# Recurrent mixer: hierarchy steps over both decays in one instruction, prefix sums in place, double tiles in turn

## The chip, the cores and the metric

The kernel runs on one core of a Trainium2 chip, as one program launched once. The time is that of the device, in microseconds (us), from runs of the whole program. Its engines work from queues of their own: TensorE (PE, with its weight loads PEld), VectorE (DVE), ScalarE (ACT), GpSimd (POOL) and SyncE (SP), which issues transfers. They wait for each other through semaphores.

## The reference, cut to what matters

The program is an encoder trunk of two layers over 1024 tokens of width 1024. Layer 0 mixes tokens by windowed attention, layer 1 by a bidirectional gated linear recurrence (HGRN2) with 8 heads; each layer also has four heads of cross-attention and ends in a channel mixer (ConvGLU). The change touches the recurrence alone:

```python
def gla_chunked(q, k, v, log_f):            # HG_CHUNK = 16
    b = jnp.cumsum(log_f, axis=2)           # prefix sums in a chunk
    b_end = b[:, :, -1:]
    q_dec = q * jnp.exp(b)
    k_dec = k * jnp.exp(-b)
    k_end = k * jnp.exp(b_end - b)
    s = jnp.where(causal, jnp.einsum('bcthk,bcshk->bchts', q_dec, k_dec), 0.0)
    o_intra = jnp.einsum('bchts,bcshv->bcthv', s, v)
    # and then a scan over the chunks: state = decay * state + k_end^T v, o_inter = q_dec state

def mixer_hgrn2(...):
    q, i, zf, zb, gate, xq = jnp.split(u @ w_in, ...)
    f = lb + (1.0 - lb) * jax.nn.sigmoid(z)       # forget gate; its log is log_f, and k = 1 - f
    o = gla_chunked(q, k_f, v, lf_f) + flip_t(gla_chunked(flip_t(q), flip_t(k_b), flip_t(v), flip_t(lf_b)))
    o = rmsnorm(o, norm_g) * jax.nn.silu(gate)
```

## The kernel before

The recurrent mixer is the function `hgrn`. It works by head (8), and in each head by four *directions*: forward and backward, each over two halves of 512 tokens (`direction(h, r, d, b, ...)`, order (0,0), (1,1), (0,1), (1,0)). A head's 128 key channels lie on the partitions, its 512 tokens along the columns. Beside it, on PE, runs the projection of a later head (`proj`): q and the two gates by channel (`proj_fm`, 24 matmuls of 512 columns for a tile `pj`), and values with their output gates by token for two heads at once (`proj_tm`, eight tiles, emptied into `v` by DVE at L1127 and into `gs` by three ACT passes, L1105 to L1107, and a DVE product, L1129). Tiles `pj` are two in turn: the next but one can start only when a tile is empty. `fp32r` weights are split into a high and a low part by ACT (`wh`) and DVE (`wl`, L79), and each product is three matmuls (L83 to L85). Cross-attention units are strewn between (`cross`).

A direction goes like this. ACT makes the log of the gate and of k from the projection `s` (L1191 to L1195). DVE subtracts (L1196), sums prefixes within 16 tokens (`B`, L1198, a scan with a mask that restarts it), and takes the rest to the chunk's end (`R`, L1201). ACT makes EP = exp(B) and ER = exp(R) (L1205, L1206), and exp(-R) and exp(-B) for half of the columns each (L1218, L1219). Four DVE products with q and k (L1220 to L1223) fill two tiles E1 and E2 for the score blocks of 32. Then comes a hierarchy: `step(n)` makes decays over 2n tokens from those over n, one instruction for the half of ER that is earlier in each pair of blocks (L1233) and one for the half of EP that is later (L1234). After the steps of 16 and 32 tokens a tile G (of 32 and of 64) is filled, one half by POOL (L1241, EP times q), the other by DVE (L1242, ER times k). PE then makes the score blocks `pa` (L1226) from G, E1, E2 and G32: 8 matmuls of 64 columns and 24 of 32, each recorded as two. A third step follows, then POOL takes `dec` and `qin` from EP (L1259, L1261), DVE makes ER times k (L1262) and copies the masked scores (L1263), PE transposes ER (`pt`, L1272), ACT copies it (L1274), PE makes the state updates `pu` (L1277), and DVE carries the state on (L1286). After four directions `output` makes the head's result (`po`, L1301).

Tiles: a pool `early` holds five tiles `E` of 512 columns in turn, which serve as a_, L1, R, B, E1, E2, G32 and G64 of each direction, and two EP and two ER.

The order of each engine's instructions is set when the program is built, by a scheduler that reads the order of the code, priorities and its own costs. `with tc.high_priority(AHEAD)` puts the emptying of projection tiles and the score blocks ahead. When an instruction's cost or the tiles that it waits for change, the order changes on all engines.

## Time and profile before

| | us |
|---|---|
| median of three runs (2657.53 to 2662.38) | 2660.64 |
| the profiled execution | 2656.7 |
| its span, first to last instruction | 2654.6 |
| PE busy in the span | 2598.7 |
| DVE busy | 1818.1 |
| ACT busy | 1377.3 |
| POOL busy | 472.4 |
| first and last hierarchy step (L1233) of the mixer start at | 1245.9 and 1889.2 |

The mean granted TensorE clock is 0.999 of full. The profile shows one execution. A group's row gives line, engine, operation, tiles (out<-in), shape and count, then busy us, mean ns of one, and the engine's idle time before them with what ended it. In a row by source line three numbers with strokes are the shortest, the median and the longest duration in ns. Matmuls are pipelined, and their ends are modelled: in a run without a wait they start closer together than they last.

### The profile page before, as it was taken

Reading aid. Unit: us, or ns where it says so; the run is one execution under the profiler, and the core shown is the slowest. Engines: PE = TensorE matmul, PEld = TensorE weight load, DVE = VectorE, ACT = ScalarE, POOL = GpSimd, SP = SyncE. Lnnn points to the kernel's source line nnn. Section 1 sums busy time; section 2 is a strip of 40 time slices with the busy share of each in tenths; the row PEclk is TensorE's granted clock in tenths of the full one; section 3 lists DMA queues with packets and bytes.
Section 4 is the critical chain, followed back from the end, with each engine's and each line's share of the span. In section 5 each row is a group of like instructions: output and inputs, shape, how many; then the busy total and the mean of one; then the engine's idle time right before and its main releaser. Section 6 shows DMA issues by size and latency. Waiting matters only on the chain. (4 is left out here: it accounts for less than half of the span.)

```text
span 2654.6 us, 39112 instructions
## 1 busy us (share of the span) xinstructions
PE 2598.7 (98%) x14420; PEld 2184.3 (82%) x14420; DVE 1818.1 (68%) x3043; ACT 1377.3 (52%) x2503; POOL 472.4 (18%) x520
## 2 busy tenths in 40 slices
PE   8999999999999999999999999999999999999998
PEld 7888887788888888887888888888887788888887
DVE  6688886577655565478688686886757755656447
ACT  6467676545444445454465554555534444445443
POOL 0421010211111100031224131231311111110013
PEclk9999999999999999999999999999999999999999
DMA  9782232367777857674235351103437778785656
GB/s 354 246 174 58 74 91 81 107 190 192 200 202 193 209 154 257 191 251 150 84 112 150 81 128 53 52 25 100 141 105 197 194 191 211 197 202 168 224 192 238
DMA packets 195728, 425.93 MB, mean 160 GB/s; under 512 B 20048, under 2 KB 56272, under 8 KB 189904
## 3 DMA queue, kind: packets, MB, share of 16 engines
q1 hardware_dynamic: 161552, 324.06, 37.7%
q0 software_dynamic: 24544, 90.19, 16.3%
q10 hardware_dynamic: 9440, 9.19, 1.1%
q8 instruction: 113, 1.85, 0.3%
q14 instruction: 79, 0.65, 0.1%
HBM read 330.04 MB, written 116.39 MB: 168 GB/s over the span
## 5 line engine op out<-in xcount | busy, mean ns | idle before, releaser
L89 DVE TENSOR_TENSOR wl<-st,wh 128x1024 fp32r<-128x1024 f32 (+1 forms) x238 | 262.7, 1110 | 317.0 <-ACT wh L88 289.0
L88 ACT CAST wh<-st 128x1024 fp32r<-128x1024 f32 (+1 forms) x238 | 222.4, 936 | 287.2 <-PE X L592 189.7
L83 PE MATMUL pj<-uh,wh 128*128 128x512 f32 x512 | 202.8, 396 | 3.8 <-DVE q L1143 1.8
L592 PE MATMUL X<-wl,wh 128*128 128x512 f32 x528 | 204.6, 389 | 0.0
L592 PE MATMUL X<-wh,wl 128*128 128x512 f32 x528 | 204.5, 389 | 0.0
L85 PE MATMUL pj<-uh,wl 128*128 128x512 f32 x512 | 202.0, 395 | 0.0
L84 PE MATMUL pj<-ul,wh 128*128 128x512 f32 x512 | 201.9, 394 | 0.1
L592 PE MATMUL X<-wh 128*128 128x512 f32 x528 | 198.7, 390 | 1.0 <-ACT c L1006 1.0
L83 PE MATMUL pj<-wh,uh 128*128 128x384 f32 (+1 forms) x512 | 189.3, 371 | 4.7 <-DVE gs L1129 2.5
L85 PE MATMUL pj<-wh,ul 128*128 128x384 f32 (+1 forms) x512 | 187.2, 366 | 0.0
L84 PE MATMUL pj<-wl,uh 128*128 128x384 f32 (+1 forms) x512 | 186.6, 364 | 0.0
L79 DVE TENSOR_TENSOR wl<-st,wh 128x1024 fp32r<-128x1024 f32 (+1 forms) x91 | 115.2, 1272 | 29.3 <-ACT wh L78 28.6
L592 PE MATMUL V<-uh,wh 128*128 128x512 f32 x336 | 130.7, 389 | 0.0
L592 PE MATMUL V<-ul,wh 128*128 128x512 f32 x336 | 130.7, 389 | 0.0
L592 PE MATMUL V<-uh,wl 128*128 128x512 f32 x336 | 130.7, 389 | 0.0
L78 ACT CAST wh<-st 128x1024 fp32r<-128x1024 f32 (+1 forms) x97 | 97.8, 1014 | 46.1 <-PE pj L84 24.2
L592 PEld LDWEIGHTS X<-wh 128*128 128x128 f32 x528 | 99.1, 188 | 22.0 <-ACT c L1006 1.4
L83 PEld LDWEIGHTS pj<-uh,wh 128*128 128x128 f32 x512 | 96.3, 188 | 24.0 <-DVE q L1143 2.6
L592 PEld LDWEIGHTS X<-wl,wh 128*128 128x128 f32 x528 | 99.1, 188 | 20.5
L592 PEld LDWEIGHTS X<-wh,wl 128*128 128x128 f32 x528 | 99.1, 188 | 20.4
L975 POOL TENSOR_TENSOR c<-c,g 128x512 f32<-128x512 f32 x24 | 43.4, 1824 | 388.5 <-DMA st<-hid 159.7
L84 PEld LDWEIGHTS pj<-ul,wh 128*128 128x128 f32 x512 | 96.3, 188 | 18.6 <-DVE ul L89 0.4
(413 smaller groups left out, 7221.8 us busy)
## 6 DMA issues: line engine op xcount, KB each, us to landing
st<-hid SPq DMA_DIRECT2D x154, 256.0 KB, 3.0
st<-in_ffw_dram SPq DMA_DIRECT2D x108, 256.0 KB, 3.4
w2s<-in_ffw_dram POOLq DMA_DIRECT2D x24, 1024.0 KB, 8.7
st<-in_ffw_dram SPq DMA_DIRECT2D x46, 512.0 KB, 4.4
hid<-tt SPq DMA_DIRECT2D x88, 256.0 KB, 4.7
st<-w2s SPq DMA_DIRECT2D x88, 256.0 KB, 3.0
sx<-in_ffw_dram SPq DMA_DIRECT2D x84, 256.0 KB, 3.9
sy<-in_ffw_dram SPq DMA_DIRECT2D x42, 512.0 KB, 7.1
```

What stands on the lines that cost most here:

```text
L78: act.copy(h[:, :n], raw)
L79: (eng or dve).tensor_tensor(l[:, :n], raw, h[:, :n].bitcast(F32), op=ALU.subtract)
L83: pe.matmul(o, ah, bh, start=first, stop=False)
L84: pe.matmul(o, ah, bl, start=False, stop=False)
L85: return pe.matmul(o, al, bh, start=False, stop=last)
L88: act.copy(h, src)
L89: dve.tensor_tensor(l, src, h.bitcast(F32), op=ALU.subtract)
L592: last = pe.matmul(o, x, y, start=new, stop=e, skip_group_check=not first)
L975: pool.tensor_tensor(y[q][:, t, :], y[q][:, t, :], g3[:, c], op=ALU.mult)
```

## The change

Both decays of a direction, and the logs that they are made from, move into one double tile `RP` of 2 x 512 columns, ER ahead of EP; two such tiles take turns. The tiles L1 and a_ are its two halves, the scan writes where it reads, and R is written over L1 with its sign turned (L1209 takes B less its end), so that ER is exp(-R).

`across(x, n)` is an operand over both halves: the earlier half of each pair of n-blocks of ER, and then the later half of each in EP. With it a step is one instruction of 512 columns (L1234 of the new kernel) in place of two of 256. `mixed` is the matching order in E1 and E2. These are filled by two exponentials of 512 columns with opposite sign (L1214, L1215) ahead of EP and ER, which are made in place (L1216, L1217), and then by two products of 512 columns (L1218, L1219) in place of four of 256 and two exponentials of 256.

E1 with E2, and G32 with G64, are halves of double tiles `E`, two in turn. The pool takes 16 KB of a partition where it took 18.

PE has the same matmuls, POOL and SP the same instructions. DVE has 160 fewer, ACT as many as before. Every engine's order in the mixer is another. After line 1181 the new kernel's line numbers are its own; from L1234 on they are one above those of before.

```diff
-            gf = early.tile([P, 512], F32, tag="E", bufs=5, name="gf")
+            gf = early.tile([P, 2, 512], F32, tag="E", bufs=2, name="gf")[:, 0, :]
...
-            def E():
-                return early.tile([P, 512], F32, tag="E", bufs=5, name="E")
+            def pair_of(tag):
+                return early.tile([P, 2, 512], F32, tag=tag, bufs=2, name=tag)
...
+            def across(x, n):
+                return bass.AP(x.tensor, x.offset + er * n, [list(x.ap[0]), [512 + (lt - er) * n, 2], [2 * n, 256 // n], [1, n]])
+            def mixed(x):
+                return bass.AP(x.tensor, x.offset + er * 16, [list(x.ap[0]), [(lt - er) * 16, 2], [32, 16], [1, 16]])
-            a_, L1 = E(), E()
+            RP = pair_of("RP")
+            ER, EP = RP[:, 0, :], RP[:, 1, :]
+            a_, L1 = EP, ER
             act.activation(a_, k, AF.Exp, scale=-1.0)
             act.activation(L1, a_, AF.Ln, bias=1.0)
...
             dve.tensor_tensor(a_, a_, L1, op=ALU.subtract)
-            R, B = E(), E()
-            dve.tensor_tensor_scan(B[:, rev], smask, a_[:, rev], 0.0, op0=ALU.mult, op1=ALU.add)
+            dve.tensor_tensor_scan(a_[:, rev], smask, a_[:, rev], 0.0, op0=ALU.mult, op1=ALU.add)
...
-            dve.tensor_tensor(v16(R), bc(v16(B)[:, :, e:e + 1], [P, 32, 16]), v16(B), op=ALU.subtract)
-            EP = early.tile([P, 512], F32, tag="EP", bufs=2, name="EP")
-            ER = early.tile([P, 512], F32, tag="ER", bufs=2, name="ER")
-            act.activation(EP, B, AF.Exp)
-            act.activation(ER, R, AF.Exp)
+            dve.tensor_tensor(v16(ER), v16(EP), bc(v16(EP)[:, :, e:e + 1], [P, 32, 16]), op=ALU.subtract)
             pa = PA[d]
-            E1, E2 = E(), E()
...
-            act.activation(e1, Re, AF.Exp, scale=-1.0)
-            act.activation(l2, Bl, AF.Exp, scale=-1.0)
-            dve.tensor_tensor(l1, pl_, ql, op=ALU.mult)
-            dve.tensor_tensor(e2, re_, ke, op=ALU.mult)
-            dve.tensor_tensor(e1, e1, qe, op=ALU.mult)
-            dve.tensor_tensor(l2, l2, kl, op=ALU.mult)
+            EE = pair_of("E")
+            E1, E2 = EE[:, 0, :], EE[:, 1, :]
+            act.activation(mixed(E1), across(RP, 16), AF.Exp)
+            act.activation(mixed(E2), across(RP, 16), AF.Exp, scale=-1.0)
+            act.activation(EP, EP, AF.Exp)
+            act.activation(ER, ER, AF.Exp, scale=-1.0)
+            dve.tensor_tensor(E1, E1, q, op=ALU.mult)
+            dve.tensor_tensor(E2, E2, k, op=ALU.mult)
...
             def step(n):
-                pl_, pe_, rl_, re_ = parts(n)[:4]
                 e = 0 if d else n - 1
-                nb = 512 // (2 * n)
-                dve.tensor_tensor(re_, re_, bc(pl_[:, :, e:e + 1], [P, nb, n]), op=ALU.mult)
-                dve.tensor_tensor(pl_, pl_, bc(pe_[:, :, e:e + 1], [P, nb, n]), op=ALU.mult)
+                x = across(RP, n)
+                ends = bass.AP(RP.tensor, RP.offset + 512 + lt * n + e,
+                               [list(RP.ap[0]), [(er - lt) * n, 2], [2 * n, 256 // n], [0, n]])
+                dve.tensor_tensor(x, x, ends, op=ALU.mult)
+            GG = pair_of("E")
             for n in (32, 64):
                 step(n // 2)
-                G = E()
+                G = GG[:, n // 64, :]
```

More of the change, by code (lines that the diff above doesn't have):

```diff
@@ L1196, in direction @@
             dve.tensor_tensor(a_, a_, L1, op=ALU.subtract)
-            R, B = E(), E()
-            dve.tensor_tensor_scan(B[:, rev], smask, a_[:, rev], 0.0, op0=ALU.mult, op1=ALU.add)
+            dve.tensor_tensor_scan(a_[:, rev], smask, a_[:, rev], 0.0, op0=ALU.mult, op1=ALU.add)
             v16 = lambda x: x.rearrange("p (b c) -> p b c", c=16)
             e = 0 if d else 15
-            dve.tensor_tensor(v16(R), bc(v16(B)[:, :, e:e + 1], [P, 32, 16]), v16(B), op=ALU.subtract)
-            EP = early.tile([P, 512], F32, tag="EP", bufs=2, name="EP")
-            ER = early.tile([P, 512], F32, tag="ER", bufs=2, name="ER")
-            act.activation(EP, B, AF.Exp)
-            act.activation(ER, R, AF.Exp)
-            pa = PA[d]
-            E1, E2 = E(), E()
-            Bl, Be = halves(B, 16)
-            Rl, Re = halves(R, 16)
-            l1, e1 = halves(E1, 16)
-            l2, e2 = halves(E2, 16)
+            dve.tensor_tensor(v16(ER), v16(EP), bc(v16(EP)[:, :, e:e + 1], [P, 32, 16]), op=ALU.subtract)
+            pa = PA[d]
+            EE = pair_of("E")
[6 more added lines that the diff above has]
+            dve.tensor_tensor(E2, E2, k, op=ALU.mult)
             def parts(n):
                 return halves(EP, n) + halves(ER, n) + halves(q, n) + halves(k, n)
-            pl_, pe_, rl_, re_, ql, qe, kl, ke = parts(16)
-            act.activation(e1, Re, AF.Exp, scale=-1.0)
-            act.activation(l2, Bl, AF.Exp, scale=-1.0)
-            dve.tensor_tensor(l1, pl_, ql, op=ALU.mult)
-            dve.tensor_tensor(e2, re_, ke, op=ALU.mult)
-            dve.tensor_tensor(e1, e1, qe, op=ALU.mult)
-            dve.tensor_tensor(l2, l2, kl, op=ALU.mult)
             def block(c, i, j, x, y, n=32):
```

## The prediction

> **What bounds the kernel now.** I read first the busy time by stretches of the span: before, during and after the recurrent mixer (the columns are engines, then granted TensorE clock, DMA share and GB/s).

> ```profile
> core 0: us, PE busy (x) PEld busy (x) DVE busy (x) ACT busy (x) POOL busy (x), PEclk, DMA share, GB/s
> 0.00:1225.00 1225.00, 1190.89 (x5860) 1009.56 (x5860) 836.30 (x1477) 679.31 (x1256) 189.79 (x223) 1.00 0.62 180
> 1225.00:1925.00 700.00, 689.91 (x5374) 581.68 (x5375) 538.53 (x1059) 370.27 (x798) 184.71 (x194) 1.00 0.33 94
> 1925.00:2654.60 729.60, 717.89 (x3188) 593.02 (x3186) 443.30 (x509) 327.71 (x450) 97.91 (x103) 0.99 0.67 192
> ```

> The edited lines run only in the middle stretch. There PE is busy 689.9 of 700 us, VectorE (DVE) 538.5, ScalarE (ACT) 370.3. The change gives PE no matmul less, so it can directly return only the 10.1 us in which PE stands, and lose what it makes PE stand longer. The second view lists the waits of PE alone in that stretch: engine, line and tile, what it waited for, us in total, times, longest.

> ```profile
> PE pa L1226 <- POOL E L1241: 2.6, 4, 1.5
> PE pj L83 <- DVE gs L1129: 2.5, 4, 0.8
> PE pj L83 <- DVE q L1143: 1.8, 2, 1.1
> PE pj L83 <- DVE s L1148: 1.0, 1, 1.0
> PE pt L120 <- DVE ul L89: 0.9, 2, 0.6
> PE pt L1272 <- ACT ot L1331: 0.8, 1, 0.8
> PE pt L1272 <- DVE ER L1262: 0.4, 1, 0.4
> PE pu L1277 <- DVE v L1127: 0.3, 1, 0.3
> ```

> They sum to 10.3 us. Half are of two kinds: score blocks that wait for POOL's product G, whose tile is named E (2.6), and projection matmuls that wait until DVE has emptied a tile of two in turn (gs 2.5). The third view shows one such wait in order of time: start, length, instruction, idle time before it.

> ```profile
> 1425.74 0.84 DVE L1233 TENSOR_TENSOR ER<-ER,EP 128x256 f32<-128x256 f32 x1
> 1426.32 0.42 ACT L1107 ACTIVATE gs<-gs 128x256 f32<-128x256 f32 x1
> 1426.69 0.42 DVE L1234 TENSOR_TENSOR EP<-EP 128x256 f32<-128x256 f32 x1
> 1427.03 0.68 DVE L1262 TENSOR_TENSOR ER<-ER,s 128x512 f32<-128x512 f32 x1
> 1427.64 0.42 DVE L1129 TENSOR_TENSOR gs<-pj,gs 128x256 f32<-128x256 f32 x1
> 1428.20 0.47 PE L83 MATMUL pj<-wh,uh 128*128 128x512 f32 x1 [0.67 <-DVE gs L1129]
> 1428.51 0.39 PE L84 MATMUL pj<-wl,uh 128*128 128x512 f32 x1
> 1428.51 0.19 PEld L85 LDWEIGHTS pj<-wh,ul 128*128 128x128 f32 x1
> 1428.74 0.39 PE L85 MATMUL pj<-wh,ul 128*128 128x512 f32 x1
> 1428.74 0.19 PEld L83 LDWEIGHTS pj<-wh,uh 128*128 128x128 f32 x1
> ```

> ACT had gs ready at 1426.74; DVE was still in three hierarchy instructions and reached it at 1427.64, and PE stood 0.67 us. So a chain off the critical path costs PE time where it stands in front of a tile to be emptied. That, not DVE's sum, is what the change can move.

> **The change, part by part: DVE's sum.** Groups by line in the mixer: count, then busy us, mean ns.

> ```profile
> L1233 DVE TENSOR_TENSOR ER<-ER,EP 128x256 f32<-128x256 f32 x96 | 55.2, 575 | 1.1
> L1198 DVE TENSOR_TENSOR_SCAN E<-smask,E 128x512 f32<-128x512 bf16 x32 | 48.7, 1522 | 1.0
> L1234 DVE TENSOR_TENSOR EP<-EP 128x256 f32<-128x256 f32 x96 | 42.6, 444 | 2.8
> L1262 DVE TENSOR_TENSOR ER<-ER,s 128x512 f32<-128x512 f32 x32 | 21.8, 682 | 0.0
> L1220 DVE TENSOR_TENSOR E<-EP,q 128x256 f32<-128x256 f32 x32 | 13.4, 420 | 1.6 <-ACT EP L1205 1.6
> L1241 POOL TENSOR_TENSOR E<-EP,q 128x256 f32<-128x256 f32 x64 | 53.0, 828 | 289.6 <-DVE EP L1234 246.8 <-ACT gs L1105 18.5 <-ACT gs L1107 8.6
> ...
> L1233 DVE TENSOR_TENSOR ER<-ER,EP x96: 407/422/1315, 1245.9 to 1889.2; 128x256 f32<-128x256 f32 x96
> ```

> Steps: 96 pairs of 256 columns become 96 instructions of 512. By medians (422 and, within 5 ns of it, L1234) a pair is 0.84 us, the new one 0.68 (L1262, two SBUF inputs, 512 columns): 96 x 0.16 = 15 us less. By means a pair is 575 + 444 = 1.02 us and the saving 32 us. The row's minimum, median and maximum (407/422/1315) say that a minority of very long ones makes the mean. I take the median, since those long ones are waits and will find another instruction. [...] Products: four of 0.42 become two of 0.68, 0.32 x 32 = 10 us less. Together 25 us off DVE's 538.5, with 12 to 42 as bounds (instructions in a row start closer than they last, so the low end is half). The prefix sum in its own tile: no row has a scan in place, but L1233 and L1234 write where they read and are no slower than L1220, which doesn't; I take 1.5 us as before, with bounds 0.68 (a plain instruction of 512) and double, 27 us less to 49 more in all. The new operands jump between two halves 512 columns apart; no row has that. Bounds: 0.42 (free) to 0.84 (as two), so the steps save between 40 us and nothing. The steps of 32 and 64 wait as a whole for POOL's product of 0.83 us, where the ER half could go ahead before; DVE has its own half of that product meanwhile (0.42), so DVE stands or does other work for 0.41 x 64 = 26 us at most, and behind it in the queue stand the copies and products that empty tiles. All of this lies beside PE's 689.9: even 49 and 26 more leave DVE at 614 of 700.

> **ACT's sum.**

> ```profile
> L1206 ACT ACTIVATE ER<-E 128x512 f32<-128x512 f32 x32 | 20.1, 628 | 4.8 <-DVE E L1201 4.2
> L1218 ACT ACTIVATE E<-E 128x256 f32<-128x256 f32 x32 | 12.9, 404 | 0.0
> L1192 ACT ACTIVATE E<-E 128x512 f32<-128x512 f32 x32 | 20.1, 629 | 33.6 <-PE pa L1226 18.6 <-DVE ER L1262 5.8 <-DVE EP L1234 4.5
> ```

> Two exponentials of 256 grow to 512: 2 x (0.628 - 0.404) x 32 = 14 us more, 385 of 700, again beside PE. Cover gone, it would cost at most those 14. All four now stand ahead of the first step, which overwrites what they read: up to three more of 0.63 ahead of it, 1.9 us, of which the shorter products and steps win back some 0.8. The last row is the wait of the next direction's second exponential for PE's blocks (18.6 us), because its tile was one of five in turn. With double tiles that wait moves to E1's exponential, later in the chain; behind it on ACT stand the other three and the sigmoids that empty q and gs. At the 18.6 us of before PE's waits for q and gs were 4.3 in all, so I take 0 and leave the rest to the rivals. The freedom to start earlier is where the new order comes from.

> **The order.** First DVE in the value projection for heads 2 and 3 (heads counted from 0): from the copy that empties the value half of a tile (L1127) to the product that frees it (L1129). This is the place of the wait above. Before:

> ```order
> L1127 COPY v<-pj 128x2x128
> L1234 TENSOR_TENSOR EP<-EP 128x8x32
> L1242 TENSOR_TENSOR E<-ER,s 128x4x64
> L1233 TENSOR_TENSOR ER<-ER,EP 128x4x64
> L1234 TENSOR_TENSOR EP<-EP 128x4x64
> L1262 TENSOR_TENSOR ER<-ER,s 128x512
> L1129 TENSOR_TENSOR gs<-pj,gs 128x2x128
> ```

> Now, the same tile (its copy is the first row, its product the last):

> ```order
> L1127 COPY v<-pj 128x2x128
> L1243 TENSOR_TENSOR E<-RP,s 128x8x32
> L93 TENSOR_SCALAR oms<-oss 128x4
> L1127 COPY v<-pj 128x2x128
> L1129 TENSOR_TENSOR gs<-pj,gs 128x2x128
> ```

> Between copy and product stood 2.4 us of DVE work, now 1.0, which is under what ACT needs for three passes of 0.42. The other three gs waits stand likewise: 2.1, 2.8 and 1.5 us of DVE work before, 1.1, 0.7 and 0.7 now. I take 2.2 of the 2.5 us as gone. But further on in the same projection, with two directions now interleaved, it stands worse; the sixth tile there has now:

> ```order
> L1127 COPY v<-pj 128x2x128
> L1218 TENSOR_TENSOR E<-E,q 128x512
> L1219 TENSOR_TENSOR E<-E,s 128x512
> L1287 SCALAR_TENSOR_TENSOR S<-S,dec,pu 128x128 x3
> L1234 TENSOR_TENSOR RP<-RP 128x2x16x16
> L1243 TENSOR_TENSOR E<-RP,s 128x8x32
> L1203 SCALAR_TENSOR_TENSOR s<-s,RP 128x512
> L1234 TENSOR_TENSOR RP<-RP 128x2x8x32
> L1129 TENSOR_TENSOR gs<-pj,gs 128x2x128
> ```

> Eight such tiles have 4.0 to 4.9 us in between (two before). In PE's order 10 to 18 us of other matmuls stand behind the tiles of that half, so I charge 1.0 us in all.

> Second, PE at the last direction of head 2: the score block (L1226) and what stands ahead of it. Before:

> ```order
> L84 MATMUL pj<-wl,uh 128x512
> L85 MATMUL pj<-wh,ul 128x512
> L1277 MATMUL pu<-v,kT 128x128
> L1272 MATMUL pt<-ident,ER 128x128 x4
> L1226 MATMUL pa<-E 32x64 x8
> L1226 MATMUL pa<-E 32x32 x24
> ```

> Now:

> ```order
> L84 MATMUL pj<-ul,wh 128x512
> L85 MATMUL pj<-uh,wl 128x512
> L1226 MATMUL pa<-E 32x64 x8
> L1226 MATMUL pa<-E 32x32 x24
> L1278 MATMUL pu<-v,kT 128x128 x4
> ```

> The transposes that ended just ahead of the block are gone from there, and more projection stands in front. Counted from the last tile that DVE must empty ahead of G, PE had 12 projection matmuls and 1.3 us of DVE work stood against them; now 45 against 4.6. At 0.23 us from start to start (the PE rows above), with the transposes between, the cover is 7 us instead of 3. At the other three blocks that waited it rises from 3 to 5, 6 and 11. So the 2.6 us go. Four other blocks fall from 5 to 10 us of cover to 2.0 to 3.5, the size at which three of the four waits came to 1.1 us in all (2.6 less the longest, 1.5): 1.0 us back, 1.6 net.

> **Switches.** The matmul that follows the block took 0.47, the next 0.39: 0.08 for each change into a projection run. The order has 113 of these in the stage before, 103 now: 0.8 us less. The other waits, 5.3 us, hang on queue positions that are dealt anew; I take 0, between all gone and doubled.

> **Sum.** -2.2 + 1.0 - 1.6 - 0.8 = -3.6 us. The profiled execution took 2656.7 us (span 2654.6) and should take 2653.1; the median of the three runs shown is 2660.6, 3.9 above it, so the forecast is 2657.0.

> **Rivals.** *Nearly all waits go* (0.20): the shorter chain lets DVE reach q and s earlier too (1.8 + 1.0), so the 5.3 fall to 1 and neither 1.0 comes: -3.6 - 4.3 - 2.0 = -9.9, 2651. For it speaks that 7 of the 10.3 us wait for DVE; against it that ACT, which stands ahead of q, gets 14 us more.

> *The second half of each value projection stalls* (0.15): one tile needs 0.42 + 4.5 + 0.42 = 5.3 us from copy to product, and with only the other tile's last 12 matmuls behind it (12 x 0.23 = 2.8) PE would stand 2.5 us, 20 us over eight places; with half of it covered 10, so 2657 + 10 = 2667, slower. It decides once fewer than 24 projection matmuls (5.4 us) really stand in between. The order speaks against it; for it, DVE's steps now wait there for POOL's products of the same tile.

> *The mixer is not bound by PE* (0.03). The PEld rows are 0.19 long and 0.23 apart in a run without a wait: 83%, and the stage has 581.7 of 700, the same share. If there were room, the stage would follow DVE's 25 us: 2636. [...]

> *The change doesn't do what it says* (0.05): the steps cost 0.84, the DVE sum stays, and PE doesn't notice: 2660.

> **Numbers.** Forecast 0.57, its own range 2653 to 2661. A measurement here tells 0.2%, 5.3 us, from no change, so faster means under 2655.3: 0.11 of the forecast's 0.57, the first rival, the third: 0.34. Same: 0.46 + 0.05 = 0.51. Slower: 0.15. The range 2650 to 2666 takes in the first rival and the lower part of the second.

> **What would show it.** PE busy in the mixer within 1 us of 689.9; PE's waits for gs under 0.5 us in the first half of each projection; for G under 1.2; DVE 505 to 520, ACT 382 to 388; the step 0.65 to 0.72 at its median; the scan unchanged. The forecast is wrong if PE's waits in the stage sum to over 15 us or under 3, or if the other stretches move by more than 2 us.

## The result, and the profile after

The changed kernel takes 2674.93 us (median of five runs, 2671.43 to 2678.36) against 2658.57 for the kernel before on the same chip (five runs, 2657.53 to 2662.38): a ratio of 1.006, with an interval of 1.0046 to 1.0074. It is slower, and it lies above the predicted range (2650 to 2666). The profiled execution took 2673.82 us with a span of 2672.0, so 17.4 us more span than before (2654.6), at a mean granted clock of 0.996 (before 0.999).

The recurrent mixer now ends some 17 us later, so its stretch is read to 1940 us. The view by stretches of the kernel after (engines, granted TensorE clock, DMA share, GB/s):

```profile
core 0: us, PE busy (x) PEld busy (x) DVE busy (x) ACT busy (x) POOL busy (x), PEclk, DMA share, GB/s
1225.00:1940.00 715.00, 694.35 (x5369) 583.29 (x5368) 533.60 (x899) 376.42 (x799) 189.25 (x194) 0.99 0.31 91
```

PE stands for 20.6 us there, twice the 10.3 of before, and its busy time too is larger (694.4 against 689.9). The larger waits of PE in that stretch (what waits, for what: us, times, longest):

```profile
PE pj L83 <- DVE gs L1129: 6.6, 5, 1.7
PE pu L1278 <- DVE S L1287: 5.9, 2, 3.3
PE pj L83 <- DVE s L1148: 2.7, 2, 1.8
PE pt L1273 <- ACT ot L1332: 2.3, 1, 2.3
PE pt L1273 <- DVE RP L1263: 1.3, 2, 0.8
PE pa L1226 <- POOL E L1242: 0.4, 1, 0.4
```

The score blocks' wait for POOL's product G is nearly gone, as forecast (2.6 to 0.4). The projection's wait for gs grew, and a kind of wait that before did not show at all is second: the state update `pu` waits for DVE's S, twice. The longer of these two, on DVE (start, length, instruction):

```profile
1718.70 1.22 DVE L1206 TENSOR_TENSOR_SCAN RP<-smask,RP 128x512 f32<-128x512 bf16 x1
...
1720.57 0.69 DVE L1203 SCALAR_TENSOR_TENSOR s<-s,RP 128x512 f32<-128x512 f32 x1
1721.17 1.22 DVE L79 TENSOR_TENSOR wl<-st,wh 128x1024 fp32r<-128x1024 f32 x1
...
1723.52 0.68 DVE L1219 TENSOR_TENSOR E<-E,s 128x512 f32<-128x512 f32 x1
1724.12 0.34 DVE L1287 SCALAR_TENSOR_TENSOR S<-S,dec,pu 128x128 f32<-128x128 f32 x1
1724.38 1.22 DVE L1206 TENSOR_TENSOR_SCAN RP<-smask,RP 128x512 f32<-128x512 bf16 x1
1725.51 0.32 DVE L1287 SCALAR_TENSOR_TENSOR S<-S,dec,pu 128x128 f32<-128x128 f32 x1
...
1726.35 0.68 DVE L1209 TENSOR_TENSOR RP<-RP 128x512 f32<-128x512 f32 x1
1726.95 0.34 DVE L1287 SCALAR_TENSOR_TENSOR S<-S,dec,pu 128x128 f32<-128x128 f32 x1
```

Two scans stand 5.7 us apart: two directions are worked on at once, and their instructions alternate. Three S of 0.32 to 0.34 us stand among them, and the last starts at 1726.95. PE on its side (the last column is the idle time before, and for what):

```profile
1723.77 0.39 PE L85 MATMUL pj<-uh,wl 128*128 128x512 f32 x1
1727.44 2.05 PE L1278 MATMUL pu<-v,kT 128*128 128x128 f32 x8 [3.28 <-DVE S L1287]
...
1729.71 0.63 PE L84 MATMUL pj<-ul,wh 128*128 128x512 f32 x1
1730.13 0.63 PE L85 MATMUL pj<-uh,wl 128*128 128x512 f32 x1
...
1730.91 0.39 PE L84 MATMUL pj<-ul,wh 128*128 128x512 f32 x1
```

PE stood for 3.28 us because the next `pu` may not be written until S has read the last one. Then its matmuls run at about half pace: 0.63 us long and 0.42 from start to start (0.39 and 0.23 ahead of the wait), until they are back at 0.39 at 1730.91. That is the second part of the loss. The stretches of 3.4 us in which the granted clock is about one half (past the first 20 us and without one at the very end):

```profile
119.70:123.10 3.40, 3.40 (x11) 3.37 (x12) 2.09 (x5) 1.31 (x3) 0.00 (x0) 0.50 0.94 330
1389.50:1392.90 3.40, 3.40 (x10) 2.63 (x9) 3.37 (x9) 0.00 (x0) 0.85 (x2) 0.50 0.00 0
1549.90:1553.30 3.40, 3.40 (x13) 3.03 (x12) 2.35 (x3) 3.33 (x6) 0.00 (x0) 0.50 0.20 80
1560.10:1563.50 3.40, 3.03 (x11) 2.87 (x12) 2.41 (x6) 0.27 (x1) 1.27 (x1) 0.51 0.00 0
1727.40:1730.80 3.40, 3.36 (x12) 3.10 (x13) 2.68 (x7) 0.27 (x1) 0.94 (x2) 0.50 0.00 0
2034.60:2038.00 3.40, 3.40 (x9) 2.61 (x9) 1.20 (x2) 0.00 (x0) 0.00 (x0) 0.50 0.83 234
```

Six, where the kernel before has one (its row stands further down, and the last row here is its counterpart). By the granted clock of 0.50 in these rows PE does in 3.4 us the work of 1.7, an estimate, so five more cost 8.5 us. With the 10.3 us of waits that makes 18.8, against 17.4 measured: the loss is these two. Only four of the five lie in the mixer (6.8 us). The one at 119.70 lies far ahead of the edited lines: PE's order is the same in both kernels up to 1255 us, and the kernel before has the same wait of 1.20 us there, at 119.3, without such a stretch. So it is not the change's doing; with it PE comes to its first different instruction 1.1 us late. At the mixer's last transposes of `on` (1915.8 us before, 1933.1 after) it is 17.3 us late, so the mixer itself loses 16.2. The five runs of the kernel go the same way: 2671.43 us at a mean clock of 0.998, 2673.82 at 0.996, and 2674.93 to 2678.36 at 0.995.

DVE was relieved by much less than its steps were: its busy time in the stretch is 533.6 us, with 160 instructions fewer, against 538.5. Groups of the kernel after, 1225 to 1925 us: count, then busy us, mean ns, idle before; the last row by source line has shortest, median and longest ns:

```profile
L1234 DVE TENSOR_TENSOR RP<-RP 128x512 f32<-128x512 f32 x96 | 67.6, 704 | 12.8 <-ACT RP L1217 8.4 <-POOL E L1242 3.7
L1206 DVE TENSOR_TENSOR_SCAN RP<-smask,RP 128x512 f32<-128x512 bf16 x32 | 39.7, 1241 | 0.7
L1243 DVE TENSOR_TENSOR E<-RP,s 128x256 f32<-128x256 f32 x64 | 39.6, 619 | 0.8
L1219 DVE TENSOR_TENSOR E<-E,s 128x512 f32<-128x512 f32 x32 | 32.5, 1017 | 0.0
L1263 DVE TENSOR_TENSOR RP<-RP,s 128x512 f32<-128x512 f32 x32 | 28.9, 903 | 0.4
L1218 DVE TENSOR_TENSOR E<-E,q 128x512 f32<-128x512 f32 x32 | 22.6, 708 | 6.4 <-ACT E L1214 6.2
L1234 DVE TENSOR_TENSOR RP<-RP x96: 658/682/1783, 1248.6 to 1907.6; 128x512 f32<-128x512 f32 x96
```

The steps fell from 97.8 to 67.6 us, 682 ns at their median. But L1219, of the same shape as L1218, takes 1017 ns to its 708 at their means, and L1263, 682 ns before, takes 903. Their medians are 684 to 691 ns; a minority of long ones makes the means. Take as long what lasts over 1.25 times its line's median: in the trace all 41 long ones of L1233 before overlap a product G of POOL (L1241). In the kernel after, 25 of the 27 long ones of L1243 overlap POOL's G, all 8 of L1263 its `qin`, and all 10 of L1219 its sum `As`, which before met the scan (9 of its 10 long ones). So the extra time beside POOL stayed and fell on other lines: summed over all DVE instructions of the mixer, the time above the median of their line is 40.4 us before and 45.8 after.

### The profile page after: what moved, and what is told of

Same layout as the page of the kernel before. It is cut to its first block, busy times and chain, and to the rows that moved or that the text cites. A ratio compares the mean times of both kernels' runs of the same rounds, so it can differ in the third digit from the quotient of the medians.

```text
span 2672.0 us, 38934 instructions
## 1 busy us (share of the span) xinstructions
PE 2606.9 (98%) x14420; PEld 2189.6 (82%) x14420; DVE 1814.5 (68%) x2883; ACT 1382.5 (52%) x2503; POOL 475.3 (18%) x520
## 5 line engine op out<-in xcount | busy, mean ns | idle before, releaser
L89 DVE TENSOR_TENSOR wl<-st,wh 128x1024 fp32r<-128x1024 f32 (+1 forms) x238 | 263.6, 1114 | 317.5 <-ACT wh L88 296.2
L83 PE MATMUL pj<-uh,wh 128*128 128x512 f32 x512 | 205.3, 401 | 8.0 <-DVE gs L1129 4.3
L85 PE MATMUL pj<-uh,wl 128*128 128x512 f32 x512 | 203.3, 397 | 0.0
L84 PE MATMUL pj<-ul,wh 128*128 128x512 f32 x512 | 202.2, 395 | 0.1
L83 PE MATMUL pj<-wh,uh 128*128 128x384 f32 (+1 forms) x512 | 189.3, 371 | 4.6 <-DVE gs L1129 2.3
L85 PE MATMUL pj<-wh,ul 128*128 128x384 f32 (+1 forms) x512 | 187.2, 366 | 0.0
L84 PE MATMUL pj<-wl,uh 128*128 128x384 f32 (+1 forms) x512 | 186.7, 365 | 0.0
L79 DVE TENSOR_TENSOR wl<-st,wh 128x1024 fp32r<-128x1024 f32 (+1 forms) x91 | 113.9, 1260 | 22.0 <-ACT wh L78 21.5
L83 PEld LDWEIGHTS pj<-uh,wh 128*128 128x128 f32 x512 | 97.3, 190 | 28.1 <-issue 4.2
L1242 POOL TENSOR_TENSOR E<-RP,q 128x256 f32<-128x256 f32 x64 | 58.9, 921 | 338.9 <-DVE RP L1234 338.7
L592 PEld LDWEIGHTS X<-wh,wl 128*128 128x128 f32 x528 | 99.1, 188 | 20.6
L85 PEld LDWEIGHTS pj<-uh,wl 128*128 128x128 f32 x512 | 97.2, 190 | 19.3
```

What stands on the lines that cost most here:

```text
L79: (eng or dve).tensor_tensor(l[:, :n], raw, h[:, :n].bitcast(F32), op=ALU.subtract)
L83: pe.matmul(o, ah, bh, start=first, stop=False)
L84: pe.matmul(o, ah, bl, start=False, stop=False)
L85: return pe.matmul(o, al, bh, start=False, stop=last)
L89: dve.tensor_tensor(l, src, h.bitcast(F32), op=ALU.subtract)
L592: last = pe.matmul(o, x, y, start=new, stop=e, skip_group_check=not first)
```

## The experiments

All numbers are of whole runs against the kernel before on the same chip, and of one profile each. This table sums them up. PE's waits are those of the mixer; half clock is the time at a granted clock of one half, start and end left out, and behind the stroke what of it lies in the mixer; "early" counts the directions (of 31) whose scan starts on DVE before PE's score block of the direction ahead, as read from the trace.

| kernel | us | ratio (interval) | span | PE waits | half clock / in the mixer | early |
|---|---|---|---|---|---|---|
| before | 2658.6 to 2660.2 | 1 | 2654.6 | 10.3 | 3.4 / 0 | 0 |
| after | 2674.93 | 1.006 (1.0046 to 1.0074) | 2672.0 | 20.6 | 20.4 / 13.6 | 14 |
| steps_only | 2665.06 | 1.0018 (1.0009 to 1.0026) | 2664.1 | 14.5 | 10.2 / 3.4 | 0 |
| tiles_only | 2679.49 | 1.0082 (1.0068 to 1.0096) | 2677.0 | 23.1 | 23.8 / 17.0 | 11 |
| after_chained | 2662.76 | 1.0009 (1.0001 to 1.0018) | 2657.1 | 12.2 | 6.8 / 0 | 0 |
| after_singles | 2674.87 | 1.0062 (1.0050 to 1.0074) | 2678.0 | 20.6 | 27.2 / 13.6 | 14 |
| logs_in_place | 2677.07 | 1.0069 (1.0056 to 1.0082) | 2674.9 | 21.9 | 23.8 / 17.0 | 13 |
| before_redealt | 2667.62 | 1.0025 (1.0015 to 1.0036) | 2666.4 | 15.4 | 13.6 / 6.8 | 0 |
| after_s_first | 2673.02 | 1.0051 (1.0037 to 1.0064) | 2673.0 | 19.4 | 20.4 / 6.8 | 14 |
| chained_s_first | 2662.55 | 1.0009 (1.0000 to 1.0018) | 2658.0 | 11.7 | 6.8 / 3.4 | 0 |
| wide_only | 2658.43 | 0.9996 (0.9987 to 1.0005) | 2656.5 | 9.2 | 6.8 / 0 | 0 |
| after_l1_in_turn | 2670.03 | 1.0040 (1.0028 to 1.0053) | 2670.5 | 17.4 | 23.8 / 20.4 | 0 |

Span, waits, half clock and "early" are those of the one profiled execution, which can lie some us from the median beside it (after_singles 5.1 above, after_chained 3.8 below). Added waits plus half of the added time at half clock give the added span of every row to within 2 us. Half clock outside the mixer comes and goes in parts that the edits leave alone.

The theory to start from: in the kernel before, ACT's log L1 of a direction (L1192) goes into a tile E that PE's score blocks of the direction ahead still read (18.6 us of waiting in the prediction's row of ACT). In the new kernel the logs lie in `RP`, so a direction may begin before that, two are dealt to DVE alternately, and what PE waits for stands behind the work of both. The rivals: the wide instructions cost it, or any newly dealt order does.

**The steps alone.** The kernel before, with EP and ER as halves of one tile and one step instruction:

```diff
-            EP = early.tile([P, 512], F32, tag="EP", bufs=2, name="EP")
-            ER = early.tile([P, 512], F32, tag="ER", bufs=2, name="ER")
+            RP = early.tile([P, 2, 512], F32, tag="RP", bufs=2, name="RP")
+            ER, EP = RP[:, 0, :], RP[:, 1, :]
...
-                dve.tensor_tensor(re_, re_, bc(pl_[:, :, e:e + 1], [P, nb, n]), op=ALU.mult)
-                dve.tensor_tensor(pl_, pl_, bc(pe_[:, :, e:e + 1], [P, nb, n]), op=ALU.mult)
...
+                dve.tensor_tensor(x, x, ends, op=ALU.mult)
```

> The kernel before with only EP and ER side by side in one double tile and each hierarchy step one instruction of 512 columns; logs, prefix sums, the four products, the exponentials and the five tiles in turn are as before. Theory A (the double tiles let two directions interleave, and that order puts DVE's and ACT's chain work ahead of what PE waits for): PE's waits in the mixer stay near 10 us, no new stretch at half clock, 2653 to 2661. Rival B (a wide instruction holds DVE longer ahead of the copies that PE waits for, whatever the tiles): about 15 us of waits, 2664 to 2672. Rival C (any newly dealt order costs, since the old one happened to be good): anywhere from 2660 to 2675.

Measured 1.0018 (1.0009 to 1.0026). Its waits grew by 4.2 us, and a new place carries them:

```profile
PE pt L1313 <- DVE on L1309: 5.7, 4, 1.8
```

Little of the loss is here, and it sits at the tile `on` of the head's output, not at a step. The time misses the range of theory A (2653 to 2661) and lies in those of both rivals, with the some 15 us of waits that rival B gave. The runs that follow speak against B; that a newly dealt order costs something stays.

**The tiles alone.** The new kernel, with two steps, four products of 256 columns and two half exponentials again, but in the double tiles:

```diff
-            act.activation(mixed(E1), across(RP, 16), AF.Exp)
-            act.activation(mixed(E2), across(RP, 16), AF.Exp, scale=-1.0)
...
+            act.activation(e1, re_, AF.Exp)
+            act.activation(l2, pl_, AF.Exp, scale=-1.0)
...
-            dve.tensor_tensor(E1, E1, q, op=ALU.mult)
-            dve.tensor_tensor(E2, E2, k, op=ALU.mult)
...
+            dve.tensor_tensor(l1, pl_, ql, op=ALU.mult)
+            dve.tensor_tensor(e2, re_, ke, op=ALU.mult)
+            dve.tensor_tensor(e1, e1, qe, op=ALU.mult)
+            dve.tensor_tensor(l2, l2, kl, op=ALU.mult)
...
-                dve.tensor_tensor(x, x, ends, op=ALU.mult)
...
+                dve.tensor_tensor(re_, re_, bc(pl_[:, :, e:e + 1], [P, nb, n]), op=ALU.mult)
+                dve.tensor_tensor(pl_, pl_, bc(pe_[:, :, e:e + 1], [P, nb, n]), op=ALU.mult)
```

> The changed kernel with its tiles (logs, prefix sums and decays in one double tile, two in turn; E1 with E2 and G32 with G64 in double tiles, two in turn), but with the instructions of before: two steps of 256 columns, four products of 256, two exponentials of 256. Theory A: slow as the changed kernel, 2668 to 2680, pairs of directions starting under 6 us apart, PE waits 18 us or more. Rival B: near before, 2656 to 2662. Rival C: anywhere from 2660 to 2675.

Measured 1.0082 (1.0068 to 1.0096). The loss is there in full without one wide instruction, which speaks against the rival that these cost it; theory A had 2668 to 2680. Its waits lie at other tiles than those of the kernel after:

```profile
PE pj L83 <- DVE s L1148: 7.4, 5, 3.0
PE pt L1278 <- DVE RP L1268: 3.4, 2, 3.0
```

**The chain tied again.** The new kernel, with the two logs in a tile of the turn of E, so that the next direction again waits for PE's blocks, and the scan from there into EP:

```diff
-            RP = pair_of("RP")
-            ER, EP = RP[:, 0, :], RP[:, 1, :]
-            a_, L1 = EP, ER
+            LA = pair_of("E")
+            a_, L1 = LA[:, 0, :], LA[:, 1, :]
...
-            dve.tensor_tensor_scan(a_[:, rev], smask, a_[:, rev], 0.0, op0=ALU.mult, op1=ALU.add)
+            RP = pair_of("RP")
+            ER, EP = RP[:, 0, :], RP[:, 1, :]
+            dve.tensor_tensor_scan(EP[:, rev], smask, a_[:, rev], 0.0, op0=ALU.mult, op1=ALU.add)
```

> The changed kernel with all its wide instructions, but the two logs of a direction in a double tile of the E turn, so that a direction can start only when PE has read E1 and E2 of the one before, as in the kernel before; the scan writes from there into RP. Theory A: the interleaving goes, waits near 10 us, 2652 to 2661. Rival B: slow as the changed kernel, 2668 to 2678. Rival C: anywhere from 2660 to 2675.

Measured 1.0009 (1.0001 to 1.0018): of the new kernel's 0.6% some 0.5% are gone, no direction starts early, and the smallest distance of two scans is 14.9 us (5.7 after). All wide instructions and double tiles are still in it. It lies just above the range of theory A (2652 to 2661) and well under that of rival B.

**Single tiles.** The new kernel, with E1, E2, G32 and G64 as four single tiles in turn in place of two double ones:

```diff
-            EE = pair_of("E")
-            E1, E2 = EE[:, 0, :], EE[:, 1, :]
+            def E():
+                return early.tile([P, 512], F32, tag="E", bufs=4, name="E")
+
+            E1, E2 = E(), E()
...
-            GG = pair_of("E")
...
-                G = GG[:, n // 64, :]
+                G = E()
```

> The changed kernel with E1, E2, G32 and G64 in four single tiles in turn in place of double tiles; the double tile of logs and decays stays. Theory A: the early start of a direction hangs on the tile of logs and decays, so this stays slow, 2668 to 2680. If instead waiting for a whole double tile is what costs, it goes back to 2655 to 2662. Rival B: slow, 2668 to 2678.

Measured 1.0062 (1.0050 to 1.0074), the same as after: the double tiles E are not the cause.

**Only the logs moved.** The kernel before, nothing wide and nothing double, with logs, prefix sums and rests made in EP and ER, and four tiles `E` for the other four uses:

```diff
-                return early.tile([P, 512], F32, tag="E", bufs=5, name="E")
+                return early.tile([P, 512], F32, tag="E", bufs=4, name="E")
...
-            a_, L1 = E(), E()
...
+            a_, L1 = EP, ER
...
-            R, B = E(), E()
+            R, B = ER, EP
...
-            act.activation(EP, B, AF.Exp)
-            act.activation(ER, R, AF.Exp)
...
             act.activation(l2, Bl, AF.Exp, scale=-1.0)
+            act.activation(EP, B, AF.Exp)
+            act.activation(ER, R, AF.Exp)
```

> The kernel before, instruction for instruction in kind and size, with EP and ER as single tiles, two each in turn, but the logs, the prefix sums and the rest to the chunk's end made in those two tiles, so that E keeps four single tiles for E1, E2, G32 and G64. Nothing wide and nothing double is in it. Theory A (making the logs in the decays' own tiles frees a direction from PE's reading of the one before, and two directions interleave): slow, 2668 to 2682, some directions starting under 8 us apart, waits of 18 us or more. If double or wide things are needed for the loss: 2656 to 2663. Rival C (any newly dealt order costs): in between, as the next kernel.

Measured 1.0069 (1.0056 to 1.0082). The theory had 2668 to 2682, and this part of the change brings the whole loss. PE's waits, among them the gs of the new kernel:

```profile
PE pj L83 <- DVE gs L1129: 7.4, 5, 3.1
PE pt L1272 <- DVE ER L1262: 4.2, 3, 2.8
```

**The order dealt anew.** The kernel before, with the two half exponentials written ahead of the two whole ones and nothing else:

```diff
-            act.activation(EP, B, AF.Exp)
-            act.activation(ER, R, AF.Exp)
...
             act.activation(l2, Bl, AF.Exp, scale=-1.0)
+            act.activation(EP, B, AF.Exp)
+            act.activation(ER, R, AF.Exp)
```

> The kernel before with its tiles and instructions, only the two exponentials of half the columns written ahead of those that make EP and ER, so that the scheduler deals every engine's order anew. Theory A: no freedom is added, so directions start over 10 us apart, and it stays within 2656 to 2666. Rival C (the order of before was a lucky one, any other costs as much as the change did): 2668 to 2680.

Measured 1.0025 (1.0015 to 1.0036). No tile is freed and no direction starts early, and still it costs a quarter of a per cent, between the ranges of theory A (up to 2666) and of rival C (from 2668). Most of its waits are in one place:

```profile
PE pj L83 <- DVE q L1143: 8.2, 3, 6.8
```

So a new order can have a price of its own, and a part of the loss may be that. logs_in_place holds this same edit; what the moved logs add to it there is 1.0069 against 1.0025.

**S first.** The new kernel, and the tied one, with the state update under a higher priority:

```diff
-                    dve.scalar_tensor_tensor(S[:, nx, :], S[:, cg, :], dec[:, c:c + 1], pu[:, c, :],
-                                             op0=ALU.mult, op1=ALU.add)
+                    with tc.high_priority(AHEAD):
+                        dve.scalar_tensor_tensor(S[:, nx, :], S[:, cg, :], dec[:, c:c + 1], pu[:, c, :],
+                                                 op0=ALU.mult, op1=ALU.add)
```

> The changed kernel with the state update (S, line 1287) put at the high priority that the emptying of projection tiles has. In the changed kernel PE waited 5.9 us for it in two pieces, 2.6 and 3.3, each followed by 3.4 us at half clock. Theory A with the clock as its second half: those two waits and their two half-clock stretches go (5.9 + 3.4 us), if no others take their place: 2664 to 2672. If the half clock has another cause than the wait, it stays, and the time falls by 6 at most.

> The kernel with wide instructions and the logs in the E turn, with the state update at high priority too. Theory A: no interleaving, so there is nothing in front of S to remove: within 4 us of that kernel, 2656 to 2666; a time under 2653 would make it better than both kernels.

Measured 1.0051 (1.0037 to 1.0064) and 1.0009 (1.0000 to 1.0018). The first misses its range (2664 to 2672), and PE still waits 5.0 us for S there (5.9 without it): the priority did not take the wait away, so this tells nothing of what it costs, and how S could be brought forward stays open. The second is the tied kernel again.

**Everything wide, logs in the turn.** The new kernel with single tiles, and the logs in these, five in turn as before (the diff is against after_singles):

```diff
-                return early.tile([P, 512], F32, tag="E", bufs=4, name="E")
+                return early.tile([P, 512], F32, tag="E", bufs=5, name="E")
...
-            a_, L1 = EP, ER
+            a_, L1 = E(), E()
...
-            dve.tensor_tensor_scan(a_[:, rev], smask, a_[:, rev], 0.0, op0=ALU.mult, op1=ALU.add)
+            dve.tensor_tensor_scan(EP[:, rev], smask, a_[:, rev], 0.0, op0=ALU.mult, op1=ALU.add)
```

> The changed kernel's wide instructions (steps, exponentials and products of 512 columns, RP as a double tile) without the early start: the two logs of a direction are single tiles of five E in turn, beside E1, E2, G32 and G64, and the scan writes from there into RP. It is the other half of the kernel that has only the logs in place. Theory A: directions start over 10 us apart, 10 to 15 us of waits in the mixer, 2655 to 2666. Rival B (the wide instructions cost): 2668 to 2678.

Measured 0.9996 (0.9987 to 1.0005). With logs_in_place this makes a pair: the wide instructions without the moved logs are as fast as before, the moved logs without a wide instruction bring the whole loss. The steps are as short as in the new kernel (67.1 us in all), PE's waits are no more than before, and ACT again stands for PE's blocks:

```profile
PE pt L1274 <- ACT ot L1333: 2.4, 1, 2.4
...
PE pj L83 <- DVE gs L1129: 0.9, 1, 0.9
```

```profile
L1204 ACT ACTIVATE E<-E 128x512 f32<-128x512 f32 x32 | 20.2, 631 | 72.2 <-PE pa L1228 56.8 <-DVE RP L1236 7.3 <-DVE RP L1264 4.3
```

Its stretch of the mixer, for the row of the kernel before in the prediction:

```profile
1225.00:1925.00 700.00, 690.78 (x5378) 580.90 (x5377) 534.60 (x900) 379.22 (x800) 189.05 (x194) 1.00 0.32 94
```

DVE's busy time is 534.6 us against 538.5: of the 30 us off its steps only 4 are left to DVE as a whole, so this run does not show what a larger relief of DVE would be worth. It shows that the wide instructions neither gain nor cost time here, and that 56.8 us of ACT standing cost nothing.

**Half tied.** The new kernel with single tiles and L1 alone in their turn, a_ and the prefix sums still in EP (the diff is against after_singles):

```diff
-            a_, L1 = EP, ER
+            a_, L1 = EP, E()
```

> The changed kernel with the prefix sums in the decays' own tile, but the second log L1 in one of four single E tiles in turn with E1, E2, G32 and G64, so that it must wait until PE has read E1 of the direction before. Only that one wait is put back. Theory A: the early start is held by that wait alone, so 2655 to 2666, directions over 10 us apart from their second instruction on. If the place of the prefix sums is what costs, and not the early start: 2668 to 2680.

Measured 1.0040 (1.0028 to 1.0053). By the theory it should have been as fast as the tied kernel: no direction starts early, and the smallest distance of two scans is 13.4 us. It misses (2655 to 2666), and lies in the range of the other reading, that the place of the prefix sums costs, and not the early start (2668 to 2680). PE's waits are again elsewhere:

```profile
PE pu L1279 <- DVE v L1127: 5.1, 2, 2.7
PE pj L83 <- DVE gs L1129: 3.8, 5, 1.7
```

So alternating directions are not the only way to this loss. Why this order is so bad was not settled. What the runs support: the five kernels in which directions alternate lie at 1.0051 to 1.0082, the six changed ones in which they don't at 0.9996 to 1.0040. Another split has no such outlier. The six kernels whose log a_ lies in EP, so that the scan works in place, are at 1.0040 to 1.0082, and the five changed ones with a_ in a tile of the turn of E at 0.9996 to 1.0025. It is not the place of the sums, which lie in EP in wide_only and after_chained too, nor the scan's own time, which has the same median in place and apart (1224 and 1225 ns). What a_ in EP does to the order beyond the early start was not followed. So that the moved logs bring the loss is shown; how much of it is the alternation and how much a badly dealt order (up to 0.4% without any alternation) stays open. No version is clear of the kernel before on the fast side.

## Why the prediction was wrong

**The bound: right.** PE bounds the stage: it grew by what PE stood and by its half clock. The rivals that PE isn't the bound and that the change doesn't do what it says both fall: the step is one instruction of 682 ns, forecast 0.65 to 0.72, and with DVE's busy time 4.9 us down the stage did not follow it.

**DVE's and ACT's sums: right in kind.** By busy time the steps gave 30 us, near the 32 by means; by medians they gave 96 x (422 + 417 - 682) ns = 15 us, as forecast. The other 15 were the long ones that were to "find another instruction", and they did: 12.4 us came back at L1243 (425 to 619 ns) and 7.1 at L1263. That they are waits, as the prediction has it, was an estimate: the traces show that they overlap instructions of POOL. The products gain 10 us by medians, as forecast, and nothing by busy time (53.8 to 55.1 us), because L1219 has long ones. The prefix sum in place costs what it did: 1224 ns at its median against 1225, and the means (1241 and 1522) differ by the long ones. Still DVE's busy time is 533.6 us, not 505 to 520: with fewer instructions fewer overlap at their ends (0.42 us long and 0.34 apart, 0.68 long and 0.60 apart), for which the prediction had put its low end at 12, and there is more extra time beside POOL (46.3 us for 40.1 in the long ones). The four exponentials of ACT grew by 13.7 us for 14 forecast; ACT's sum of 376.4 is still under its 382 to 388, since they too start closer than they last (0.62 us long, 0.52 apart).

**G: right.** 1.6 us of net gain forecast, 2.2 came.

**The gs waits: wrong.** "I take 2.2 of the 2.5 us as gone" and "I charge 1.0 us in all" make -1.2; measured +4.1 (2.5 to 6.6). Of the four places named for the first term three are indeed free of it, the fourth grew from 0.67 to 1.71, and another tile of the first halves has 0.61. And the charge for the second half of the projections was too small: three waits there make 4.3 us, 0.93, 1.69 and 1.69, each at the last of the eight tiles of a projection. The step that failed is "10 to 18 us of other matmuls stand behind the tiles of that half". The last tile of one, on DVE and then on PE (the first PE row is the last matmul into the tile):

```profile
1808.33 2.34 DVE L79 TENSOR_TENSOR wl<-st,wh 128x1024 fp32r<-128x1024 f32 x2
1810.59 0.41 DVE L1127 COPY v<-pj 128x256 f32<-128x256 f32 x1
1810.93 1.21 DVE L79 TENSOR_TENSOR wl<-st,wh 128x1024 fp32r<-128x1024 f32 x1
...
1813.28 1.78 DVE L1219 TENSOR_TENSOR E<-E,s 128x512 f32<-128x512 f32 x1
...
1815.58 0.41 DVE L1129 TENSOR_TENSOR gs<-pj,gs 128x256 f32<-128x256 f32 x1
```

```profile
1806.39 0.39 PE L85 MATMUL pj<-wh,ul 128*128 128x512 f32 x1
...
1814.07 0.39 PE L85 MATMUL pj<-uh,wl 128*128 128x512 f32 x1
1816.14 0.47 PE L83 MATMUL pj<-uh,wh 128*128 128x512 f32 x1 [1.69 <-DVE gs L1129]
```

From copy to the end of the product 5.4 us pass, as the order let expect (4.0 to 4.9 and the two ends). But the tile is full at 1806.8, and DVE starts the copy 3.8 us later, behind splits of weights (L79) and the product of the tile before; that lateness the prediction did not count. So the tile takes 9.2 us to become free, and PE has 7.7 us of work for that time, not 10 to 18. At the other two waits it is 7.2 us against 6.4, and 9.2 against 7.7. The second rival, a stall in that half, would have come with "fewer than 24 projection matmuls" in between. Here 24 stand behind the tile, of which 15 are left when the copy starts. Its stall came, at three places and for 4.3 us, for another reason than its own. That its time, 2667, was nearer than the forecast's is luck: the rest of the loss has nothing to do with it.

**"The other waits, 5.3 us, hang on queue positions that are dealt anew; I take 0, between all gone and doubled": the step that failed most.** They came to 13.6 us, +8.3: S 5.9, where before no wait for S shows, s 2.7, ot 2.3, RP 1.3. That is 2.6 times, past the doubling that was taken as the bound without a row for it, and the 0 was a choice between two bounds, not a working. The order that the prediction itself quoted showed the risk: three S in a row in the midst of another direction's products and steps. S was not followed to PE, which stood for up to 3.28 us until S had read the last `pu`.

**The clock: a term that the sum did not have.** +6.8 us from four stretches at half clock in the mixer, each beside a wait of 1.8 to 3.3 us; the prediction counted a wait of PE at its own length. In terms, for the mixer: gs +4.1, G -2.2, other waits +8.3, clock +6.8, together 17.0, less the 0.8 forecast for switches (not measured apart) 16.2, and 16.2 measured. The two waits for S with the two stretches beside them are 9.3 of it, the largest part. The rest of the 17.4 lies ahead of the mixer, where nothing was changed. The prediction's own mark for being wrong, waits over 15 us in the stage, was met.

**The reason given for a new order: named, and taken as neutral.** "The freedom to start earlier is where the new order comes from" points at the part of the change, the moved logs, that the pair wide_only and logs_in_place shows to bring the loss. Whether the early start itself is what costs stays open.

## What to carry to other kernels

Where one engine is full, an edit to the others is worth what it does to that engine's waits: 30 us off one line of DVE left 4 us to DVE and nothing to the program, and moving the logs into other tiles cost 0.7%, a reordering that came with it included. When tiles are freed the order is dealt anew, and it can be a worse one, so before freeing a tile, list what the full engine waits for (every tile that it must get back, small state updates too) and count what now stands ahead of each, from the moment the tile is full, and how much work the full engine has left that doesn't need that tile. Price a long wait of TensorE above its length: each stretch of 3.4 us at half clock that came with one here cost 1.7 us more, by the estimate above.

## What the runs showed of the hardware

**Beside a wait of PE of 2 us the clock often halves for 3.4 us.** Over the profiles of the twelve kernels, without start and end, and with the same places counted in each kernel, 12 of 14 waits over 2.4 us lie just ahead of or in a stretch at half clock, 20 of 40 between 1.7 and 2.4, and 10 of 79 between 1.1 and 1.7; no such stretch is without a wait of at least 0.8 us beside it, and some last 6.8 us. The same wait does not always come with it. In the stage after the mixer every kernel waits alike at one place; this row of the kernel before stands alike in after_chained:

```profile
PE Y L592 <- ACT wh L78: 2.2, 1, 2.2
```

The stretch behind it, before and then in after_chained (the number ahead of the DMA share is the granted clock):

```profile
2015.60:2019.00 3.40, 3.25 (x8) 2.28 (x9) 2.88 (x4) 1.04 (x2) 0.00 (x0) 0.50 0.62 151
```

```profile
2016.30:2019.70 3.40, 3.15 (x11) 2.02 (x12) 2.78 (x4) 0.93 (x1) 0.00 (x0) 1.00 0.72 169
```

**The extra time beside POOL stayed when the instructions that had it went.** With two steps made one, the means of L1243 grew by 46% and of L1263 by 32%, and L1219 takes 44% more than its twin L1218 (groups above), at medians of 426, 691 and 686 ns (418 and 681 before, 684 for L1218). There are 74 long DVE instructions in the mixer, before as after; each of them overlaps an instruction of POOL, and together they lie 40.1 us above their medians before and 46.3 after. The product of 1.78 us that starts at 1813.28 runs beside a sum of POOL up to 1814.51, and so do the other long ones of L1219:

```profile
1812.87 1.64 POOL L1270 TENSOR_TENSOR As<-As,Az 128x512 f32<-128x512 f32 x1 [5.88 <-DVE Az L1264]
```
